# The layer's opening stage: token norm and first projections put into the kernel's own instruction order, with the gain pre_g multiplied on VectorE

## The chip, the cores and the metric

One core of a Trainium2 chip runs the whole layer. The metric is the device time of one execution in microseconds (us). Engines are named as in the profile: PE is TensorE, DVE VectorE, ACT ScalarE, POOL GpSimd, SP the engine that issues the DMAs.

## What is computed

2064 tokens (16 meta tokens and 2048 of x, 1024 wide) are normalised, projected into six streams, and run through eight heads of stick-breaking attention beside a gated linear recurrence (RG-LRU). Both groups are normalised, gated and projected back.

```
u = rmsnorm(concat(meta, x), pre_g)
q, k, v, g_att, x_lru, g_lru = split(u @ w_in)
z = q k^T / sqrt(128);  w = exp(log_sigmoid(z) + sum over later keys of log(1 - sigmoid(z)))
att = rmsnorm(w v, att_out_g) * silu(g_att)
xc = causal conv of width 4 over x_lru;  r, i = sigmoid(block gates of xc)
a = exp(8 r log_sigmoid(lambda));  h_t = a_t h_(t-1) + sqrt(1 - a_t^2) i xc
lru = rmsnorm(h, lru_out_g) * silu(g_lru)
out = x + rmsnorm(concat(att, lru) @ w_out, post_g)
```

## The kernel before

**Number format.** Every float32 operand of a matmul is split into two float16 parts, high and low, and a product is three matmuls (high by high, high by low, low by high). A projection of one 128-column block of `w_in` over n tokens is therefore 24 matmuls of n columns (8 slices of the 1024-wide sum, three products each), into one PSUM bank of the pool `psm`, which has three. `uH` and `uL` hold the normalised tokens transposed (feature on the partition), for the whole run.

**Opening stage.** The tokens come in a tile of the 16 meta tokens and 16 tiles of 128. `norm_tile` loads a tile by DMA; ACT squares it with a row sum and takes a square root (L192, L193); DVE inverts that (L194); POOL multiplies the tile by the scaled gain `pgt` (L195); ACT writes the high part, scaled by the inverse (L197), and DVE the low part (L198). The first four tiles are transposed on PE, into a PSUM tile `z` for both halves, and copied out by ACT (L205) and DVE (L206); the other 13 go through two DMA transposes each (L208, L209). `load_w` brings a weight block: DMA, a column maximum on DVE (L144, L147), a small PE matmul that spreads it over the partitions (L150), five small DVE instructions (L151 to L156), the high part on ACT (L158), the low part on DVE (L159).

Four weight blocks are needed first: k0, v0, q0 of attention head 0, and xl0, the recurrence input of channel block 0. The tokens are projected in five pieces (`KV_CH`: 144, 384, and three of 512) for k, v and q, and in six pieces of 344 for xl0. `Mix` is the recurrence of one channel block in two halves of 1032 tokens: a convolution (DVE, four instructions), six gate steps (ACT cast L485, DVE subtraction L486, two PE matmuls L496 and L497, two ACT sigmoids L498 and L499), then tanh, two exponentials, a square root, a multiply on POOL, a scan on DVE, and a square. In the opening stage the first half of block 0 is run by `lru_mix` when the last token piece is due; the second half comes later, with head 0's attention.

**What sets the order.** The opening stage is written in program order, and the framework's scheduler chooses the order of PE, ACT and DVE instructions by its own estimates. From the line `with tc.manual_schedule(...)` on, the order of these three engines is the one in which the kernel's own planner emits them: `Plan` keeps a clock per engine, `Ring` counts free buffers, `Chunk` is one projection piece, `weave` picks what PE does next (a list of urgent steps, then attention outputs, then attention scores, then the projection pieces in the list `fill`), and callbacks emit what follows on ACT and DVE. POOL's and SP's queues are set by the framework throughout. Before the planner starts, the weight blocks xl1, ga0 and gl0 are already converted (they were prefetched inside the last token piece); the planner's loader then has one raw buffer `wraw` and three converted pairs `wH`, `wL`.

Attention of a head: PE computes scores into `z` (two PSUM buffers), ACT takes the sigmoid (L305), POOL masks the diagonal (L310), DVE scans (L315), ACT and DVE split the result (L327, L333), a DMA transposes it, and PE multiplies it with v (L352).

Of the kernel before, what the change touches and what calls it, by code (L numbers as in the profile page):

```python
# [19 lines left out]
P = 128  # L20
# [50 lines left out]
def hybrid_layer(nc, tc, I, out):  # L71
# [3 lines left out]
    PE_T = 400  # L75
# [40 lines left out]
    pgt = rp.tile([P, 1036], F32, name="lrow")[:, :D]  # L116
# [13 lines left out]
    def load_w(col, home=None, raw=None):  # L130
# [11 lines left out]
        sp.dma_start(out=raw, in_=I["w_in"][col])  # L142
        m = sm.tile([P, 4], F32, name="wm", bufs=6)
# [6 lines left out]
        pe.matmul(out=ps[:, :P], lhsT=onesb, rhs=dg, start=True, stop=True)  # L150
        dve.tensor_reduce(out=m[:, 1:2], in_=ps[:, :P], axis=AX.X, op=ALU.max)  # L151
# [6 lines left out]
        act.activation(out=wH, in_=raw, func=AF.Copy, scale=m[:, 3:4])  # L158
        dve.scalar_tensor_tensor(out=wL, in0=raw, scalar=m[:, 3:4], in1=wH, op0=ALU.mult, op1=ALU.subtract)  # L159
        yield wH, wL, m[:, 2:3]  # L160

    def proj(w, c0, n):

        for ps in proj_steps(w, c0, n):
            pass
        return ps
# [18 lines left out]
    early_rows = [acc_l[:, 0:D], acc_l[:, D:2 * D]]  # L185

    def norm_tile(src, rows, t0):
        xt = early_rows.pop(0) if early_rows else frow()
        x2 = sg.tile([P, 1024], F32, name="w", bufs=N_W) if t0 // P % 2 else sg.tile([P, 1024], F32, name="wT", bufs=3)
        sp.dma_start(out=xt[:rows, :D], in_=src)  # L190
        ss = sm.tile([P, 1], F32, name="ss")
        act.activation(out=x2[:rows, :D], in_=xt[:rows, :D], func=AF.Square, accum_out=ss[:rows])  # L192
        act.activation(out=ss[:rows], in_=ss[:rows], func=AF.Sqrt, bias=eps[:rows], scale=1.0 / D)  # L193
# [6 lines left out]
        if t0 < PE_T:  # L200
            z = psz.tile([P, 2, 512], F32, name="z").bitcast(F16).rearrange("p a (k c) -> p a k c", k=KT)
            for x, t in enumerate((xh, xl)):
                for k in range(KT):
                    pe.transpose(out=z[:, x, k, :rows], in_=t[:rows, k * P:(k + 1) * P], identity=ident[:rows, :rows])
            act.copy(out=uH[:, :, t0:t0 + rows], in_=z[:, 0, :, :rows])  # L205
            dve.tensor_copy(out=uL[:, :, t0:t0 + rows], in_=z[:, 1, :, :rows])  # L206
            return
        sp.dma_start_transpose(uH[:, :, t0:t0 + rows], xh[:rows])  # L208
        sp.dma_start_transpose(uL[:, :, t0:t0 + rows], xl[:rows])  # L209


# [4 lines left out]
    def pair(ps, n, hi, lo):  # L216

        act.activation(out=hi, in_=ps[:, :n], func=AF.Copy, scale=PSC)
        dve.scalar_tensor_tensor(out=lo, in0=ps[:, :n], scalar=PSC, in1=hi, op0=ALU.mult, op1=ALU.subtract)  # L219

    def k_chunk(h, w, j, ps=None):
        if j == 0:
            kqv["kH"] = kp.tile([P, T], F16, name="kH")
            kqv["kL"] = kp.tile([P, T], F16, name="kL")
        c0, n = KV_CH[j]
        pair(ps or proj(w, c0, n), n, kqv["kH"][:, c0:c0 + n], kqv["kL"][:, c0:c0 + n])

    def q_chunk(h, w, j, ps=None):
        if j == 0:
            kqv["qH"] = kp.tile([P, S], F16, name="qH")  # L230
            kqv["qL"] = kp.tile([P, S], F16, name="qL")
        c0, n = KV_CH[j]
        if j == 0:
            c0, n = NM, n - NM
        pair(ps or proj(w, c0, n), n, kqv["qH"][:, c0 - NM:c0 - NM + n], kqv["qL"][:, c0 - NM:c0 - NM + n])

    def v_chunk(h, w, j, ps=None):


        if j == 0:  # L240
            kqv["v"] = kp.tile([P, NB, P], F16, name="v")
            kqv["vb"] = sm.tile([P, NQ], F32, name="vb", bufs=2)
            kqv["vl"] = sm.tile([P, len(KV_CH)], F32, name="vl", bufs=2)
            kqv["vu"] = unscale(w, 1.0 / VSC)
        v = kqv["v"]
        c0, n = KV_CH[j]
        a = acc_a[:, 0:1040] if h == 0 else frow()
        if j == 0:
            pool.memset(a[:, 0:1], 0.0)
        else:  # L250
            dve.tensor_copy(out=a[:, 0:1], in_=kqv["vl"][:, j - 1:j])
        act.activation(out=a[:, 1:n + 1], in_=(ps or proj(w, c0, n))[:, :n], func=AF.Copy, scale=VSC)
        dve.tensor_copy(out=kqv["vl"][:, j:j + 1], in_=a[:, n:n + 1])
        d = a[:, 520:520 + n]
        pool.tensor_tensor(out=d, in0=a[:, 0:n], in1=a[:, 1:n + 1], op=ALU.subtract)
        t = stage("sv").bitcast(F16).rearrange("p (x c) -> p x c", x=2)
        act.copy(out=t[:, 0, :n], in_=d)
        dve.tensor_tensor(out=t[:, 1, :n], in0=d, in1=t[:, 0, :n], op=ALU.subtract)
        o = 0
        if j == 0:  # L260
            tm = sm.tile([P, P], F16, name="tm", bufs=1)
            pool.memset(tm[:, 3 * NM:], 0.0)
            for x, y in enumerate((0, 0, 1)):
                dve.tensor_copy(out=tm[:, x * NM:(x + 1) * NM], in_=t[:, y, 0:NM])
            sp.dma_start_transpose(v[:, 0:1, :], tm)
            o = NM
        b0, nb = (c0 + o - NM) // P, (n - o) // P
        dve.tensor_scalar(out=kqv["vb"][:, b0:b0 + nb].unsqueeze(2),
                          in0=a[:, 1 + o:1 + n].rearrange("p (b c) -> p b c", c=P)[:, :, P - 1:P],
                          scalar1=kqv["vu"], scalar2=None, op0=ALU.mult)  # L270
        for x in range(2):
            sp.dma_start_transpose(v[:, 1 + x * NQ + b0:1 + x * NQ + b0 + nb, :], t[:, x, o:n])
# [86 lines left out]
    def attend(i, zs, o):  # L359
        pred = None  # L360
        for x in tile_segs(i):
            x.pred, pred = pred, x
            x.scores()
            x.products_1(zs)
            if x.si == 0:
                x.mask()
            x.products_2()
            x.split_1()
            x.split_2()
            x.split_3()  # L370
            x.output(o)

    def silu(ps, n, w, tag):

        g = stage(tag)
        act.activation(out=g[:, :n], in_=ps[:, :n], func=AF.Sigmoid, scale=w)
        dve.scalar_tensor_tensor(out=g[:, :n], in0=ps[:, :n], scalar=w, in1=g[:, :n], op0=ALU.mult, op1=ALU.mult)
        return g

# [14 lines left out]

    def att_gate_early(h, g, w, us):

        sp.dma_start(out=aa_d[g][h], in_=silu(proj(w, NM + 512 * g, 512), 512, us, "sa"))

    def att_gate(h, g, w, us, ot, gt=None, ps=None):
        if w is None:  # L400
            gt = gt or stage("sa")
            sp.dma_start(out=gt, in_=aa_d[g][h])
        else:
            gt = silu(ps or proj(w, NM + 512 * g, 512), 512, us, "sa")
        dve.scalar_tensor_tensor(out=gt, in0=ot, scalar=prm(ATG, h), in1=gt, op0=ALU.mult, op1=ALU.mult)
        sp.dma_start(out=aa_d[g][h], in_=gt)
# [40 lines left out]
    def lru_x(c, m, w, us, xs, ps=None):  # L447
# [9 lines left out]
        ps = ps or proj(w, half * HT + a, n)  # L457
        act.activation(out=xs[half][:, 3 + a:3 + a + n], in_=ps[:, :n], func=AF.Copy, scale=us)

    class Mix:  # L460
# [3 lines left out]
        def __init__(self, c, xs, gw, left=None):  # L464
# [81 lines left out]
    def lru_mix(c, xs, gw, left=None):  # L546
# [6 lines left out]
        for f in (mix.tanh, mix.exp_a, mix.exp_a2, mix.rest, mix.sqrt, mix.drive, mix.recur, mix.square, mix.add):  # L553
            for m in range(len(xs)):
                f(m)
# [1039 lines left out]
```

## Time and profile before

| | |
|---|---|
| median of 3 runs | 1898.63 us (1898.0 to 1902.92) |
| profiled execution | 1900.03 us, span of its instructions 1898.2 us |
| PE, DVE, ACT, POOL busy | 1796.1, 1280.7, 1043.8, 407.9 us |
| mean granted TensorE clock | 0.991 |
| longest PE line | projections, L174: three groups of about 620 us |
| last projection of k0, v0, q0, xl0 ends | 163.7 us |
| first scores of head 0, 1, 2 | 118.4, 341.1, 518.4 us |

The span is what the profile's rows cover. A granted clock of 1.0 is the full 2.4 GHz, 0.5 is 1.2 GHz. PE busy and PE idle together give the span; as PE is nearly always busy after the first 220 us, the question in a stage is what PE waits for there.

### The profile page before, as it was taken

The page shows a single profiled execution, that of the slowest core. Times are in us where ns is not written, and L with a number is a line of the kernel's source. Part 1 is how long each engine was busy: PE and PEld are TensorE (multiplying, and loading weights), DVE is VectorE, ACT ScalarE, POOL GpSimd, SP SyncE. Part 2 cuts the span into 40 slices and gives each one's busy share as a digit, 9 for nine tenths or more (in the row PEclk, how much of TensorE's full clock was granted, in tenths as well). Part 3 has the DMA queues.
Part 4 walks back from the last instruction along what each step waited for, and adds up shares of the span by engine and source line. Part 5 has one row for each costly group of instructions (what it writes and reads, how often), then busy time and mean ns, then how long its engine had stood idle before and what let it go on. Part 6 is the DMA issues. An engine that isn't in the chain of part 4 may idle for free.

```text
span 1898.2 us, 30853 instructions
## 1 busy us (share of the span) xinstructions
PE 1796.1 (95%) x12048; PEld 1151.8 (61%) x12048; DVE 1280.7 (67%) x1752; ACT 1043.8 (55%) x1775; POOL 407.9 (21%) x460
## 2 busy tenths in 40 slices
PE   2878899999999999999999999999999999999998
PEld 2434565466556655665566566556655578888776
DVE  8446886788588758866886798588757852124554
ACT  5555846756665575567456656665674743233221
POOL 4421200511140132104111411150123000002222
PEclk9989999999999999999999999999999999999999
DMA  5922561264146406631652265137404774355554
GB/s 165 199 50 58 105 130 39 62 139 92 46 96 127 95 24 130 122 73 32 131 115 62 54 136 107 54 74 140 95 30 94 197 177 138 105 163 170 177 184 138
DMA packets 435809, 205.29 MB, mean 108 GB/s; under 512 B 370368, under 2 KB 404160, under 8 KB 435664
## 3 DMA queue, kind: packets, MB, share of 16 engines
q1 hardware_dynamic: 435664, 203.33, 46.0%
q8 instruction: 94, 1.54, 0.3%
q14 instruction: 51, 0.42, 0.1%
HBM read 78.23 MB, written 34.08 MB: 59 GB/s over the span
## 4 chain that ended last, share of the span: by engine, by line
PE 73%; DVE 8%; ACT 6%; DMA 6%; issue 5%; POOL 2%; SPq 1%; DVEq 0%; POOLq 0%; ACTq 0%
PE mm L174 39%; PE y L728 18%; PE o L352 8%; PE z L301 6%; DMA wT<-w 4%; DVE row L315 2%; ACT row L305 1%; DVE lrow L531 1%; DMA wraw<-in_w_in 1%; PE mm L496 1%; DVE w L333 1%; ACT lrow L499 1%; ACT w L327 1%; ACT ot L385 1%; DMA row<-in_x 1%
## 5 line engine op out<-in xcount | busy, mean ns | idle before, releaser
L174 PE MATMUL mm<-uH,wH 128*128 128x512 f16 (+3 forms) x1808 | 620.0, 347 | 8.1 <-DVE qL L219 4.5
L174 PE MATMUL mm<-uL,wH 128*128 128x512 f16 (+3 forms) x1808 | 619.7, 346 | 2.3 <-DMA uL<-w 1.5
L174 PE MATMUL mm<-uH,wL 128*128 128x512 f16 (+3 forms) x1808 | 618.6, 346 | 2.7 <-DVE wL L159 2.7
L174 PEld LDWEIGHTS <-wH 128*128 128x128 f16 x3616 | 335.5, 99 | 287.2 <-issue 21.1
L315 DVE TENSOR_TENSOR_SCAN row<-row 128x656 f32<-128x656 f32 (+6 forms) x208 | 341.4, 1642 | 69.3 <-POOL row L310 39.8
L174 PEld LDWEIGHTS <-wL 128*128 128x128 f16 x1808 | 178.2, 99 | 164.2 <-issue 6.1
L305 ACT ACTIVATE row<-z,zs 128x656 f32<-128x656 f32 (+6 forms) x208 | 171.3, 826 | 166.7 <-PE z L301 151.6
L352 PE MATMUL o<-wT,v 128*128 128x128 f16 x3392 | 223.8, 219 | 22.0 <-DMA wT<-w 20.8
L352 PEld LDWEIGHTS <-v 128*128 128x128 f16 x3392 | 205.8, 98 | 63.0 <-issue 29.9
L333 DVE TENSOR_TENSOR w<-row,w 128x640 f16<-128x640 f32 (+5 forms) x208 | 176.2, 849 | 5.4 <-ACT w L327 5.3
L327 ACT CAST w<-row 128x640 f16<-128x640 f32 (+5 forms) x208 | 155.3, 747 | 25.9 <-DVE row L315 22.3
L310 POOL TENSOR_SCALAR_AFFINE_SELECT row<-row 128x128 f32<-128x128 f32 x128 | 88.9, 695 | 264.9 <-ACT row L305 256.7
L728 PE MATMUL y<-woH,aH 128*128 128x512 f32 x352 | 140.2, 398 | 2.0 <-DVE w L333 1.4
L728 PE MATMUL y<-woL,aH 128*128 128x512 f32 x352 | 138.0, 392 | 1.0 <-DVE woL L681 1.0
L728 PE MATMUL y<-woH,aL 128*128 128x512 f32 x352 | 138.1, 392 | 0.5 <-DVE aL L721 0.5
L301 PE MATMUL z<-kH,qH 128*128 128x328 f16 (+10 forms) x384 | 122.6, 319 | 7.6 <-ACT row L305 7.5
L301 PE MATMUL z<-kH,qL 128*128 128x328 f16 (+10 forms) x384 | 122.5, 319 | 0.0
L301 PE MATMUL z<-kL,qH 128*128 128x328 f16 (+10 forms) x384 | 122.5, 319 | 0.0
L323 POOL MEMSET w<- 128x80 f16 x128 | 21.2, 165 | 438.8 <-DMA wT<-w 331.2
L301 PEld LDWEIGHTS <-qH 128*128 128x128 f16 x768 | 72.0, 98 | 58.3 <-issue 11.2
L486 DVE TENSOR_TENSOR cs<-lrow,cs 64x344 fp32r<-64x344 f32 x96 | 49.1, 511 | 85.2 <-ACT cs L485 83.4
L1541 POOL TENSOR_TENSOR row<-row 128x512 f32<-128x512 f32 x32 | 46.5, 1454 | 261.5 <-ACT row L1540 253.6
(208 smaller groups left out, 2539.2 us busy)
## 6 DMA issues: line engine op xcount, KB each, us to landing
wraw<-in_w_in SPq DMA_DIRECT2D x46, 512.0 KB, 4.0
row<-in_x SPq DMA_DIRECT2D x31, 512.0 KB, 4.3
aa_d<-sa SPq DMA_DIRECT2D x34, 256.0 KB, 2.1
al_d<-sl SPq DMA_DIRECT2D x32, 256.0 KB, 2.7
araw<-in_w_out SPq DMA_DIRECT2D x16, 512.0 KB, 4.5
araw<-al_d SPq DMA_DIRECT2D x16, 512.0 KB, 4.3
yl_d<-ys SPq DMA_DIRECT2D x32, 256.0 KB, 2.2
row<-yl_d SPq DMA_DIRECT2D x16, 512.0 KB, 3.2
```

Of the source, the lines that this page charges most:

```text
L174: pe.matmul(out=ps[:, :n], lhsT=a[:, kt, :], rhs=b[:, kt, c0:c0 + n], start=(k == 0), stop=(k == 3 * KT - 1))
L301: pe.matmul(out=z[:, a, :n], lhsT=l[:, qs], rhs=r[:, c], start=(x == 0), stop=(x == 2))
L305: act.activation(out=self.om[:, :L].rearrange("p (a c) -> p a c", a=self.parts), in_=self.z[:, :self.parts, :self.n], func=AF.Sigmoid, sca ...
L310: pool.affine_select(out=d, in_=d, pattern=[[-1, P]], compare_op=ALU.is_gt, fill=1.0, base=0, channel_multiplier=1)
L315: dve.tensor_tensor_scan(out=om, data0=om, data1=om, initial=self.pred.om[:, 0:1] if self.si else WS, op0=ALU.mult, op1=ALU.bypass)
L323: pool.memset(w[:, 3 * NM:P], 0.0)
L327: act.copy(out=w[:, r0:r0 + nb * P], in_=om[:, self.m0:self.L])
L333: dve.tensor_tensor(out=w[:, r0 + nb * P:r0 + 2 * nb * P], in0=om[:, self.m0:self.L], in1=w[:, r0:r0 + nb * P], op=ALU.subtract)
L352: pe.matmul(out=o[:, c], lhsT=l, rhs=r, start=(self.si == 0 and x == 0), stop=(self.last and x == len(prods) - 1))
L486: dve.tensor_tensor(out=cs[oth, :n], in0=xc[own, a:a + n], in1=cs[own, :n], op=ALU.subtract)
L728: pe.matmul(out=ps, lhsT=a[:, c, :], rhs=b[:, 512 * half:512 * half + 512], start=(c == 0 and x == 0), stop=(c == KT - 1 and x == 2))
L1541: pool.tensor_tensor(out=yt[:, cs], in0=yt[:, cs], in1=pg[:, cs], op=ALU.mult)
```

## The change

The planner now starts at the first instruction. Its parts:

- **Norm on DVE.** `norm` replaces `norm_tile`. The gain is scaled once on ACT (L473, on POOL before). DVE multiplies the tile by inverse norm and gain in one instruction, in float32 and in place (L695); ACT casts the high part (L697), DVE subtracts (L700). POOL has no part in it.
- **Transposes.** The high part of 12 tiles (meta, 0 to 5, 7, 9, 11, 13, 15) and the low part of three (meta, 0, 1) go over PE, each half with a `z` tile of its own (L722, copied at L724). The other 19 go by DMA (L715). That is 120 PE transposes, 64 before.
- **Order.** ACT and DVE steps of norm and weights go through `job`, which emits, of what is ready, the tile with the lowest number first; weights v0, q0, xl0 stand among the tiles at 1.5, 2.5 and 4.5. A projection piece may start when the planner thinks that its tokens are there (`have`).
- **First LRU mix whole.** xl0 is an ordinary branch now: both halves of block 0 run their gates among the last projections, and the rest of both during head 0's attention. `lru_mix`, `prefetch` and the split into two calls are gone.
- **Decay constants.** The chain of small DVE instructions of `decay` (L418 to L434 before) is emitted when the planner's clock is at 45, and not in the first microseconds.
- **Weights.** Raw tiles of v0, q0, xl0 lie in `lrow` buffers and xl0's converted pair too (`lx`); k0, v0 and q0 hold the three converted pairs. So xl1, ga0 and gl0 are converted by the loader, one after the other, after the first of k0, v0, q0 has been used up.
- **Fill order of head 0.** All pieces of k0, v0, q0 and xl0 by token, then the four of ga0, then xl1 and gl0.

```diff
-    PE_T = 400
+    PE_HI, PE_LO = set(range(-1, 6)) | {7, 9, 11, 13, 15}, {-1, 0, 1}
-    pgt = rp.tile([P, 1036], F32, name="lrow")[:, :D]
+    pgt = acc_a[:, 0:D]
-    pool.tensor_scalar(out=pgt, in0=pgt, scalar1=gm[:, 3:4], scalar2=0.0, op0=ALU.mult, op1=ALU.add)
+    act.activation(out=pgt, in_=pgt, func=AF.Copy, scale=gm[:, 3:4])
-    def norm_tile(src, rows, t0):
...
-        dve.reciprocal(out=ss[:rows], in_=ss[:rows])
-        pool.tensor_tensor(out=xt[:rows, :D], in0=xt[:rows, :D], in1=pgt[:rows], op=ALU.mult)
-        xh, xl = x2.bitcast(F16)[:, :D], x2.bitcast(F16)[:, D:2 * D]
-        act.activation(out=xh[:rows], in_=xt[:rows, :D], func=AF.Copy, scale=ss[:rows])
-        dve.scalar_tensor_tensor(out=xl[:rows], in0=xt[:rows, :D], scalar=ss[:rows], in1=xh[:rows],
-                                 op0=ALU.mult, op1=ALU.subtract)
+            def scale():
+                dve.reciprocal(out=ss[:rows], in_=ss[:rows])
+                dve.scalar_tensor_tensor(out=x, in0=x, scalar=ss[:rows], in1=pgt[:rows], op0=ALU.mult, op1=ALU.mult)
+            J("act", t, 1.55, f, lambda t: J("dve", t, 1.4, scale, lambda t: J(
+                "act", t, 1.05, lambda: act.copy(out=d["h"], in_=x), hi)), "sqrt")
+        def hi(t):
+            J("dve", t, 1.22, lambda: dve.tensor_tensor(out=d["l"], in0=x, in1=d["h"], op=ALU.subtract), lo)
+            if i in PE_HI:
+                urgent.append((t, rz, lambda: turn(uH, "h", 0)))
+            else:
+                across(uH, "h", t)
...
+        def turn(u, a, e):
+            z = psz.tile([P, 2, 512], F32, name="z").bitcast(F16)[:, 0].rearrange("p (k c) -> p k c", k=KT)
+            for k in range(KT):
+                pe.transpose(out=z[:, k, :rows], in_=d[a][:, k * P:(k + 1) * P], identity=ident[:rows, :rows])
...
+        plan.at(45.0, lambda: (decay(), V(A(plan.free["pe"], 8, "exp"), 4500)))
...
+            if ready[self.name] > plan.free["pe"] or not have(self.c0, self.n):
...
         if h == 0:
-            return GA[:2] + XL[:3] + GL + XL[3:] + GA[2:]
+            first = branch(0) + [x for j in range(NJ) for x in (K[j], VV[j], Q[j])]
+            first.sort(key=lambda x: next(j for j, (a, n) in enumerate(KV_CH) if x.c0 + x.n <= a + n))
+            return first + GA + XL[:3] + GL + XL[3:]
...
-    for name in ("xl1", "ga0", "gl0"):
-        ready[name] = 0.0
-        rW.n -= 1
-    head[0] = {"v": [0.0] * NQ, "q": 0.0, "mix": Mix(0, xs[1:], gw, hs[0]), ...}
+    lx = row()
     with tc.manual_schedule(engines={mybir.EngineType.PE, mybir.EngineType.Activation, mybir.EngineType.DVE}):
-        loader()
-        rlrow.get(lambda: mix_start(0, 0))
+        start()
         weave()
```

How the instructions stand now is shown at three places. Names: `wm` and `dg` belong to a weight's scale, `ss` to a tile's norm, `pol` and `s` to the decay constants, `cs` to a gate step.

DVE, from the first weight's scale to the second token tile, before:

```order
L147 TENSOR_SCALAR dg<-identb,wm 128x128
L615 RECIPROCAL gm<-gm 128x1
L427 TENSOR_TENSOR pol<-pol,s_527 128x8
L194 RECIPROCAL ss<-ss 16x1
L428 TENSOR_SCALAR pol<-pol 128x8
L151 TENSOR_REDUCE wm<-mm 128x1
...
L144 TENSOR_REDUCE wm<-lrow 128x1
...
L159 SCALAR_TENSOR_TENSOR wL<-wraw,wm,wH 128x1024
L147 TENSOR_SCALAR dg<-identb,wm 128x128
L428 TENSOR_SCALAR pol<-pol 128x8
...
L144 TENSOR_REDUCE wm<-lrow 128x1
...
L198 SCALAR_TENSOR_TENSOR wT<-acc_l,ss,wT 16x1024
```

and in the change:

```order
L149 TENSOR_SCALAR dg<-identb,wm 128x128
L472 RECIPROCAL gm<-gm 128x1
...
L694 RECIPROCAL ss<-ss 16x1
L695 SCALAR_TENSOR_TENSOR acc_l<-acc_l,ss,acc_a 16x1024
L163 SCALAR_TENSOR_TENSOR wL<-wraw,wm,wH 128x1024
...
L695 SCALAR_TENSOR_TENSOR acc_l<-acc_l,ss,acc_a 128x1024
L700 TENSOR_TENSOR w<-acc_l,w 16x1024
...
L695 SCALAR_TENSOR_TENSOR acc_a<-acc_a,ss 128x1024
...
L700 TENSOR_TENSOR wT<-acc_l,wT 128x1024
L700 TENSOR_TENSOR w<-acc_a,w 128x1024
L146 TENSOR_REDUCE wm<-lrow 128x1
L149 TENSOR_SCALAR dg<-identb,wm 128x128
```

The decay chain (L427, L428) and the second and third weight's maximum (L144) stood between the first tiles; now the first three tiles' multiply and subtraction follow each other, with the second weight's maximum behind them.

PE, from the last token piece to the scores of head 0, before:

```order
L174 MATMUL mm<-uH,lrow 128x344
L496 MATMUL mm<-cs_1003,gH 128x344
L497 MATMUL mm<-cs_1003,gL 128x344
L301 MATMUL z<-kH,qH 128x144
...
L496 MATMUL mm<-cs_1012,gH 128x344
L497 MATMUL mm<-cs_1012,gL 128x344
L496 MATMUL mm<-cs_1020,gH 128x344
L497 MATMUL mm<-cs_1020,gL 128x344
L496 MATMUL mm<-cs_1028,gH 128x344
L497 MATMUL mm<-cs_1028,gL 128x344
...
L174 MATMUL mm<-uH,wH 128x512
```

and in the change (the last rows of a projection, then a gate step, a further piece of it, and the end of all projections):

```order
L174 MATMUL mm<-uH,wL 128x512
L379 MATMUL mm<-cs_1220,gH 128x344
L380 MATMUL mm<-cs_1220,gL 128x344
L174 MATMUL mm<-uH,wH 128x512
...
L379 MATMUL mm<-cs_1223,gH 128x344
L380 MATMUL mm<-cs_1223,gL 128x344
...
L174 MATMUL mm<-uH,wL 128x512
L152 MATMUL mm<-dg,onesb 128x128
L379 MATMUL mm<-cs_1256,gH 128x344
L380 MATMUL mm<-cs_1256,gL 128x344
L219 MATMUL z<-kH,qH 128x144
```

Before, the gate steps of the first half stand in one row, one behind the other, ahead of the last token piece of k, v and q. Now each stands alone among the projection matmuls, eight ahead of the first scores' place and four around them.

ACT, from the first scores of head 0 to the high part of ga0's weight, in the change:

```order
L223 ACTIVATE row<-z,zs 128x144
L161 ACTIVATE wH<-wraw,wm 128x1024
L381 ACTIVATE row<-mm,pp 64x344
...
L223 ACTIVATE row<-z,zs 128x400
...
L390 ACTIVATE row<-row,nsp 128x1032 x2
...
L393 ACT_TABLE_LOAD
L393 ACTIVATE lrow<-row,nsp_m 128x1032
L223 ACT_TABLE_LOAD
L223 ACTIVATE row<-z,zs 128x528
L397 ACT_TABLE_LOAD
L397 ACTIVATE row<-row,nsp_m_76 128x1032
L161 ACTIVATE wH<-wraw,wm 128x1024
```

The high part of ga0 (the last row) comes behind the tanh of both halves and two exponentials of the first, with table loads between them. Before, ga0 had been converted ahead of the first of these sigmoids but one.

## Rows read from the trace of the kernel before

**Rows 1.** The page: busy time of each engine, and PE's busy tenths in 40 slices.

```profile
PE 1796.1 (95%) x12048; PEld 1151.8 (61%) x12048; DVE 1280.7 (67%) x1752; ACT 1043.8 (55%) x1775; POOL 407.9 (21%) x460
...
PE   2878899999999999999999999999999999999998
```

**Rows 2.** Busy time by stretch; the columns stand in the first line.

```profile
core 0: us, PE busy (x) PEld busy (x) DVE busy (x) ACT busy (x) POOL busy (x), PEclk, DMA share, GB/s
0.00:35.49 35.49, 5.06 (x51) 3.99 (x52) 29.85 (x62) 19.13 (x31) 17.39 (x19) 1.00 0.46 169
35.49:97.40 61.91, 48.55 (x308) 29.58 (x307) 37.84 (x71) 35.53 (x63) 31.27 (x16) 0.94 0.90 188
...
118.40:164.00 45.60, 31.51 (x139) 15.43 (x139) 18.82 (x33) 24.88 (x35) 7.67 (x6) 0.81 0.14 41
164.00:220.00 56.00, 48.98 (x374) 31.42 (x372) 41.99 (x53) 49.60 (x84) 16.70 (x22) 1.00 0.33 58
...
341.11:518.38 177.27, 168.56 (x1250) 102.52 (x1249) 138.86 (x181) 110.74 (x187) 44.10 (x48) 1.00 0.42 90
```

**Rows 3.** What PE waited for until 164 us: us in total, times, longest.

```profile
PE mm L150 <- DVE dg L147: 28.6, 4, 11.4
PE mm L496 <- DVE cs L486: 5.2, 4, 3.2
...
PE mm L174 <- DVE qL L219: 4.5, 1, 4.5
```

**Rows 4.** Timeline of POOL: start us, us, instruction, idle time before it and its releaser.

```profile
9.62 4.64 POOL L195 TENSOR_TENSOR acc_l<-acc_l,lrow 16x1024 f32<-16x1024 f32 x2
17.35 4.88 POOL L195 TENSOR_TENSOR row<-row,lrow 128x1024 f32<-128x1024 f32 x2 [3.10 <-ACT w L192]
```

**Rows 5.** Timeline of DVE, 0 to 40 us.

```profile
3.66 0.17 DVE L423 TENSOR_TENSOR s<-y 128x8 f32<-128x8 f32 x1
...
9.91 4.38 DVE L428 TENSOR_SCALAR pol<-pol 128x8 f32<-128x8 f32 x1
...
16.42 1.28 DVE L159 SCALAR_TENSOR_TENSOR wL<-wraw,wm,wH 128x1024 f16<-128x1024 f32 x1
17.61 2.34 DVE L147 TENSOR_SCALAR dg<-identb,wm 128x128 bf16<-128x128 bf16 x1
...
23.57 1.27 DVE L198 SCALAR_TENSOR_TENSOR wT<-acc_l,ss,wT 16x1024 f16<-16x1024 f32 x1
```

**Rows 6.** Timeline of ACT, 0 to 40 us.

```profile
6.98 1.05 ACT L192 ACTIVATE wT<-acc_l 16x1024 f32<-16x1024 f32 x1 [4.00 <-DMA acc_l<-in_meta]
...
8.21 1.28 ACT L193 ACT_TABLE_LOAD   x1
9.51 0.29 ACT L193 ACTIVATE ss<-ss,eps 16x1 f32<-16x1 f32 x1
...
17.18 1.13 ACT L197 ACTIVATE wT<-acc_l,ss 16x1024 f16<-16x1024 f32 x1
```

**Rows 7.** Timeline of PE: the first projection matmul.

```profile
35.49 0.33 PE L174 MATMUL mm<-uH,wH 128*128 128x144 f16 x1
```

**Rows 8.** Chain that ended last, 130 to 170 us: start us, us, what.

```profile
141.65 3.73 DMA wraw<-in_w_in
...
150.04 1.30 DVE wL L159
151.35 3.64 DMA wraw<-in_w_in
...
166.10 1.94 PE mm L174 x9
```

**Rows 9.** Timeline of ACT: the two sigmoids of a gate step.

```profile
120.11 0.54 ACT L498 ACTIVATE row<-mm,pp 64x344 f32<-64x344 f32 x1
120.67 0.54 ACT L499 ACTIVATE lrow<-mm,pp 64x344 f32<-64x344 f32 x1
```

**Rows 10.** Timeline of PE: a wait among head 0's scores.

```profile
205.03 0.30 PE L301 MATMUL z<-kH,qH 128*128 128x320 f16 x1 [2.86 <-ACT row L305]
```

More of the change, by code (lines that the diff above doesn't have):

```diff
@@ L214, in hybrid_layer @@
     kqv = {}
[L216 to L272, printed above, removed]
@@ L357, in tile_segs @@
         return [Seg(i, si, *t, len(segs)) for si, t in enumerate(segs)]
[L359 to L378, printed above, removed]
     def att_out(h, g, o, vsc):
@@ L393, in att_out @@
         return ot
[L395 to L406, printed above, removed]
     HT = T // 2
@@ L779, in due, with job, end, ready @@
             while self.todo and self.todo[0][0] <= self.free["pe"]:
-                heapq.heappop(self.todo)[2]()
-        def flush(self):
-            while self.todo:
-                t, _, f = heapq.heappop(self.todo)
-                self.free["pe"] = max(self.free["pe"], t)
-                f()
+                self.t, _, f = heapq.heappop(self.todo)
+                f()
+        def job(self, e, prio, t, us, f, then, table=None):
+            def end(t):
+                t = self.run(e, t, us, table)
+                self.at(t, lambda: then(t))
+            if prio is None:
+                f()
+                end(t)
+                return
+            def ready():
+                heapq.heappush(self.jobs[e], (prio, self.n, f, end))
+                self.n += 1
+                self.at(max(self.free[e], self.t), lambda: self.pick(e))
+            self.at(t, ready)
+        def pick(self, e):
+            if not self.jobs[e]:
+                return
+            if self.free[e] <= self.t + 0.01:
+                _, _, f, end = heapq.heappop(self.jobs[e])
+                f()
+                end(self.t)
+            self.at(self.free[e], lambda: self.pick(e))
     plan = Plan()
@@ L830, in loader, with mm @@
-        rW.get(lambda: rraw.get(raw_free))
+        parts = load_w(ctile[name[:-1]] + int(name[-1]), home, raw)
+        next(parts)
+        J = lambda e, t, us, then: plan.job(e, prio, t, us, lambda: next(parts), then)
+        t = (LD if prio is None else LDX)(plan.free["pe"])
+        plan.at(t, lambda: J("dve", t, 1.45, lambda t: urgent.append((t + (3.0 if prio is None else 0.0), rmm, mm))))
+        def mm():
+            next(parts)
+            J("dve", PE(0, 128), 1.2, lambda t: (rmm.put(t), J("act", t, 1.1, lambda t: J("dve", t, 1.25, end))))
@@ new lines, in have, with start @@
+    def have(c0, n):
+        return all(ut.get(i, 1e9) <= plan.free["pe"] for i in range((c0 - NM) // P, (c0 + n - NM - 1) // P + 1))
+    def start():
+        rrow.n -= 2
+        homes.extend(frow() for _ in range(2))
+        rW.n -= 3
+        rraw.n -= 1
+        weight(None, None, rraw.put, -2)
+        norm(-1)
+        rlrow.n -= 4
+        for i in range(3):
+            weight(lx if i == 2 else None, row(), rlrow.put, (1.5, 2.5, 4.5)[i])
+        plan.at(45.0, lambda: (decay(), V(A(plan.free["pe"], 8, "exp"), 4500)))
+        loader()
@@ L833, in hybrid_layer, with __init__ @@
     class Chunk:
-        def __init__(self, name, c0, n, then, gate=None, first=None, last=False):
+        def __init__(self, name, c0, n, then, gate=None, first=None, last=False, home=None):
             self.name, self.c0, self.n, self.then, self.gate, self.first, self.last = name, c0, n, then, gate, first, last
+            self.home = home or rW
             self.steps = None
@@ L1158, in recur @@
             if m + 1 == n:
-                head[c]["hs"] = ([mix.left] if n == 1 else []) + mix.xcs
+                head[c]["hs"] = mix.xcs
             plan.at(t, lambda: square(m))
```

218 lines of the change are left out of this document (87 added, 131 removed).

## The prediction, made before the changed kernel was run

> **What bounds the kernel now.** I read the page first [rows 1]: PE is busy 95% of the span, and of its 40 slices of 47 us only the first four stand clearly below nine tenths. The end is set by PE's work and by what PE loses in the first 220 us. The table by stretch [rows 2] says where: 5.06 us busy of the first 35.49, then 48.55 of 61.91, 31.51 of the 45.60 up to the last projection of k0, v0, q0 and xl0, and 48.98 of the next 56.00. The idle times add up to 30.4 + 13.4 + 14.1 + 7.0 = 65 us, and the granted clock is 0.94 and 0.81 in the second and third, so that part of the busy time there is at 1.2 GHz. In the steady stretch of head 1 PE misses only 8.7 of 177.
>
> PE's waits [rows 3] name VectorE: 28.6 us in four waits for `dg`, the step that spreads a weight's maximum, 5.2 us for the gate steps' `cs`, 4.5 us for one `qL`. The timelines of POOL and DVE, side by side [rows 4, 5], tell why `dg` is late. POOL's gain multiply takes 4.64 us for two tiles. An eight-element DVE instruction that starts 0.3 us after them takes 4.38 us and ends with them, where the same kind takes 0.17 alone, and `dg` takes 2.34 us beside the next two. So DVE is busy 29.85 us of the first 35.49 without having 29.85 us of work.
>
> **The change part by part.** All sums are made against the profiled execution, 1900.0 us, which is 1.4 us above the median of the runs.
>
> *Start.* The first projection matmul stands at 35.5 us [rows 7]. In the change, ACT ends the meta tile's root at 9.8 and scales the gain, 1.1 us like its other 1024-element instructions [rows 6]: 10.9. Up to k0's first piece, DVE then has eight instructions of 1024 elements (three multiplies, three subtractions, k0's low part, v0's maximum). Such an instruction keeps DVE for 1.2 us, from L159's start to the next one's [rows 5]: 9.6 us, and with `dg` and the copies of three low transposes some 11. ACT has eight of 1.1 us beside it. First projection at about 22: 13 us earlier.
>
> The new multiply itself (float32 out, two tensors and a scalar in) has no row. The nearest is L198, with the same operands and 1.27 us [rows 5]; the far end is POOL's rate, 2.32 us [rows 4]. I take 1.2 from start to start. At the far end 17 tiles cost another 19 us of DVE. Multiply and subtraction at 1.2 each are 41 us for 17 tiles; the four weights need 13, convolution, gate splits, evictions and copies 28, the decay chain of 31 small instructions 6 (0.17 each plus a gap): 88 us of DVE until the projections end. They end after 130 us by the sum below, so DVE has room as a whole, though not at the start.
>
> *Up to xl0.* From 22 us DVE has 14 long instructions (three more maxima and low parts among norm steps of tiles 2 to 6) before xl0's low part is there: 17 us, with three groups of small scale instructions 3, evictions 1.5, and some 4 us of waits for ACT and PE in queue order. xl0's first piece starts at about 47. PE does only the 144-token pieces and transposes until then.
>
> *The projections.* From there PE is the bound. Left are 1920 columns of each of k0, v0, q0 and 2064 of xl0, 24 matmuls per column; nine matmuls of 512 take 1.94 us [rows 8], 0.42 ns a column: 79.2 us. Five blocks of eight transposes are 2.2 and eight gate steps 2.3. (All 56 added transposes are 3.0 us of PE.) For a low clock at first and for waits in queue order I add 5. The last projection ends at 47 + 89 = 136, not 163.7: 28 us earlier. Tokens are not late: the last tile's subtraction is due near 87 by DVE's queue without waits, with some 4 us for its DMA transpose behind it, and PE wants it at about 115. SP's loads of tiles 7 on stand behind these transposes, which this slack covers. The decay chain now falls at about 50, beside k0's and v0's 384-token pieces; without that cover it would cost its 6 us.
>
> *A wait comes new.* The pieces of ga0 follow, and ga0 is not converted yet. xl1's small PE matmul stands behind the last projection (the order shows it), so its low part ends near 139 and only then is the raw buffer free. ga0's load takes 3.7 us [rows 8], maximum and scale 2.5: 145.5. Its high part stands on ACT behind the rest of the gate steps (two sigmoids of 0.54 each [rows 9]), head 0's first sigmoids and splits, two tanh and two exponentials of 1.1, and three table loads of 1.28 [rows 6]: 15 us from 138, so 153, and with high and low part 155.5. PE has 5 us of attention and gates in these 19. Without ACT's share it would be 149: two conversions follow each other at about ten us in the rows [rows 8]. Before, ga0's first matmul stood at 163.7, so 8 us are left; and by then PE has done the second half's six gate steps (1.7 us) and 3.4 us more of attention. That makes 13 us ahead.
>
> *Behind it.* The 7.0 us idle of 164 to 220 [rows 2] come from ACT's table loads for the second half, one wait of 2.86 us for a sigmoid among them [rows 10]. In the change more of these loads fall into the wait for ga0, and four ga0 pieces of 5.2 us are there to run. I leave 2 us: 5 saved. From head 1's end on the order of PE has as many instructions per head as before; nothing changes.
>
> Sum: 13 + 5 = 18 us. 1900.0 - 18 is 1882 for a profiled execution, **1880 us** for the median.
>
> **A rule against it.** Rows first: in the opening stage DVE is the helper with most to do [rows 2], and this change puts 17 multiplies of 1.2 us on it. The Trainium skill, Perfetto Trace Analysis, section Optimizing Scalar/DVE Operations, says that a saturated DVE may be relieved by giving work to ScalarE or even GpSimd, though it warns that those two share a port. By the first half of that rule the change goes the wrong way: it is rival 1. By the second half the move out of GpSimd costs DVE less than it looks. The trace agrees with the second half in the two stretched instructions above; no run yet shows the first.
>
> **The rivals.**
> 1. *VectorE sets the pace.* If DVE's queue rather than PE is the limit throughout, the 17 x 1.2 = 20 us lie on the path and eat the gain: 1880 + 20 = 1900, no change. For it: PE already waits for DVE in all of [rows 3], and up to xl0 DVE is the limit. Against it: 88 us of work in 130.
> 2. *Slower: the gate steps hold PE.* PE's queue now has 12 gate steps singly among projections and first scores, each behind an ACT cast and a DVE subtraction that stand in line with the norm of the last tiles. A late `cs` stops the projections behind it. The longest such wait was 3.2 us [rows 3]; 12 of them are 38 us, 35 beyond what the sum holds: 1915. At 2.3 us per step the result would be slower by over 0.3%. Against it: four of them cost 5.2 in all, and projection matmuls stand between as cover.
> 3. *ga0 is in time.* If ACT takes ga0's high part without that delay, at 149, the sum gains 6.5: 1873.5; with no waits in queue order among the projections either, 1868.5; and with nothing lost behind it, 1866. Against it: the order on ACT is fixed.
> 4. *Half of it.* The start's alternation of ACT and DVE costs more than the few us that I gave it, xl0 comes at 56 and not 47: 1889. The change doing less than it says is excluded by the order.
>
> **How the numbers follow.** Forecast 0.52, rival 1 0.12, rival 2 0.09, rival 3 0.18, rival 4 0.09. A measurement of this kernel can tell about 0.3% (5.7 us) from no change. Faster by more: the forecast and rivals 3 and 4, 0.79; same: rival 1, 0.12; slower: rival 2, 0.09. The range runs from rival 3's far end, with 3 us for the start, to rival 1: 1863 to 1900; it leaves out rival 2 and less than that below.
>
> **What would show it.** First projection matmul near 22 us, xl0's first piece near 47, last projection near 136, ga0's first matmul near 155 with a gap of over ten us before it, no DVE instruction of eight elements beyond half a us in the first 40 us, and the scores of head 2 some 18 us before 518.4. Wrong would be: PE waits for `cs` beyond 20 us in sum, DVE without idle time up to the last projection, or a head later than the second that takes longer than before.

## The result, and the profile after

| | before | after |
|---|---|---|
| median | 1899.24 us (1898.0 to 1902.92, 4 runs) | 1883.22 us (1882.76 to 1883.62, 4 runs) |
| profiled execution | 1900.03 us | 1882.98 us |
| span of its instructions | 1898.2 us | 1881.1 us |
| first scores of head 0, 1, 2 | 118.4, 341.1, 518.4 us | 134.7, 316.1, 495.9 us |

The ratio is 0.9912, with a 95% interval of 0.9895 to 0.993. The page of the changed kernel, busy time of each engine and PE's busy tenths:

```profile
PE 1795.0 (95%) x12104; PEld 1155.2 (61%) x12104; DVE 1282.7 (68%) x1759; ACT 1047.9 (56%) x1789; POOL 343.3 (18%) x442
...
PE   3987999999999999998999899999999999999998
```

Against [rows 1] POOL lost 64.6 us of busy time, DVE gained 2.0, and PE is busy 1.1 us less, with 56 more transposes. So 16.0 of the 17.1 us by which the span got shorter are time in which PE stood idle before. The table by stretch shows where it still does, the columns as in [rows 2]:

```profile
0.00:20.00 20.00, 3.56 (x40) 2.92 (x40) 12.97 (x23) 13.18 (x19) 1.41 (x12) 1.00 0.84 303
20.00:40.00 20.00, 10.39 (x111) 8.92 (x109) 18.26 (x41) 17.43 (x32) 0.62 (x3) 0.80 0.50 126
40.00:60.00 20.00, 15.79 (x95) 9.39 (x96) 17.96 (x53) 15.61 (x25) 0.29 (x1) 0.77 0.57 143
60.00:80.00 20.00, 20.00 (x126) 11.48 (x125) 17.29 (x21) 12.31 (x21) 1.41 (x1) 1.00 1.23 231
80.00:100.00 20.00, 17.93 (x98) 9.82 (x97) 8.41 (x15) 17.55 (x30) 1.30 (x3) 1.00 0.16 34
100.00:120.00 20.00, 19.69 (x113) 10.72 (x113) 8.66 (x10) 10.50 (x18) 4.12 (x3) 1.00 0.28 54
120.00:140.00 20.00, 17.02 (x85) 8.27 (x82) 11.07 (x20) 12.65 (x24) 1.33 (x2) 1.00 0.07 14
140.00:160.00 20.00, 9.78 (x53) 5.84 (x54) 13.54 (x25) 18.52 (x27) 4.68 (x8) 0.66 0.29 78
```

There are two holes. One is the first 60 us, where DVE is busy 18 of 20 from 20 us on. The other is 140 to 160, where PE misses 10.2 us, ACT is busy 18.5 of 20, and the granted clock is 0.66. The longest of PE's waits from 0 to 220 us name the same things (us in total, times, longest):

```profile
PE mm L152 <- DVE dg L149: 13.1, 3, 8.3
PE z L722 <- ACT w L697: 12.6, 4, 5.8
PE o L270 <- DMA wT<-w: 8.1, 3, 5.1
PE mm L379 <- DVE cs L369: 3.2, 2, 2.0
```

The 28.6 us for `dg` of [rows 3] are 13.1, and the gate steps' 5.2 are 3.2, although all twelve now run before 141 us and only six did before 164. The steps that the prediction named, on PE's timeline of the changed kernel: the first projection, xl0's first piece (its first two matmuls need only the high part and stand at 43.20; it goes on at 46.00, when the low part is there), head 0's first scores (right after the last projection), two attention outputs, and ga0's first matmul:

```profile
21.55 0.32 PE L174 MATMUL mm<-uH,wH 128*128 128x144 f16 x1
...
46.00 0.75 PE L174 MATMUL mm<-uH,lrow 128*128 128x344 f16 x2 [2.05 <-DVE lrow L163]
...
134.73 0.24 PE L219 MATMUL z<-kH,qH 128*128 128x144 f16 x1
...
145.88 0.58 PE L270 MATMUL o<-wT,v 128*128 128x128 f16 x4 [5.06 <-DMA wT<-w]
...
151.82 1.22 PE L270 MATMUL o<-wT,v 128*128 128x128 f16 x10 [2.17 <-DMA wT<-w]
...
155.75 0.39 PE L174 MATMUL mm<-uH,wH 128*128 128x512 f16 x1 [1.07 <-ACT wH L161]
```

So the front came as the working had it. What the working did not have lies behind head 2. Here are the stretches from one head's first scores to the next, heads 2 to 4 of the kernel before and then of the changed one (columns as above):

```profile
518.38:696.75 178.37, 176.62 (x1296) 106.51 (x1294) 137.17 (x189) 109.78 (x191) 39.35 (x51) 1.00 0.44 90
696.75:875.41 178.66, 176.63 (x1296) 106.45 (x1294) 136.28 (x189) 109.42 (x191) 39.34 (x51) 1.00 0.44 90
875.41:1056.47 181.06, 178.15 (x1297) 107.26 (x1295) 136.21 (x189) 109.67 (x191) 39.07 (x51) 0.99 0.43 89
```

```profile
495.91:674.96 179.05, 176.23 (x1296) 106.74 (x1295) 136.82 (x189) 107.77 (x188) 36.74 (x51) 1.00 0.43 90
674.96:857.77 182.81, 178.64 (x1296) 107.07 (x1295) 138.84 (x188) 106.97 (x188) 37.45 (x51) 0.99 0.43 88
857.77:1039.72 181.95, 176.40 (x1295) 106.63 (x1294) 136.97 (x190) 107.76 (x188) 35.70 (x50) 1.00 0.45 89
```

The number of PE instructions in a head is the same but for one or two, the time is not. At head 2 the changed kernel leads by 518.38 - 495.91 = 22.5 us. At head 7 it leads by 1414.10 - 1400.18 = 13.9, so 8.6 are gone, and the tail (484.1 before, 480.9 after) gives 3.2 back: 17.1 in the span. PE idles 20.0 us in heads 2 to 6 of the changed kernel and 11.1 in those of the kernel before, so the loss is idle time. It can be seen on PE's timeline of the changed kernel, in heads 3 and 4, all the idle times over 1.2 us:

```profile
703.45 0.72 PE L270 MATMUL o<-wT,v 128*128 128x128 f16 x10 [1.97 <-DMA wT<-w]
710.36 1.07 PE L270 MATMUL o<-wT,v 128*128 128x128 f16 x16 [1.75 <-DMA wT<-w]
...
886.01 0.89 PE L270 MATMUL o<-wT,v 128*128 128x128 f16 x13 [2.08 <-DMA wT<-w]
892.93 1.07 PE L270 MATMUL o<-wT,v 128*128 128x128 f16 x16 [2.79 <-DMA wT<-w]
```

An attention output reads `wT`, the weights that a DMA has transposed. Before, there is one such wait per head (at 726.96 in head 3, 1.45 us), now there are two. Half of what head 3 alone loses is something else: PE is busy 2.0 us longer in it, at a granted clock of 0.99. From 704.4 us, behind the wait of 1.97, the clock stands at 0.5 for 3.4 us. The kernel before has the same dip in head 4 (178.15 busy).

### The profile page after: what moved, and what is told of

Its sections match the earlier page's. It is cut to its first block, busy times and chain, and to the rows that moved or that the text cites. A ratio compares the mean times of both kernels' runs of the same rounds, so it can differ in the third digit from the quotient of the medians.

```text
span 1881.1 us, 30861 instructions
## 1 busy us (share of the span) xinstructions
PE 1795.0 (95%) x12104; PEld 1155.2 (61%) x12104; DVE 1282.7 (68%) x1759; ACT 1047.9 (56%) x1789; POOL 343.3 (18%) x442
## 5 line engine op out<-in xcount | busy, mean ns | idle before, releaser
L174 PEld LDWEIGHTS <-wH 128*128 128x128 f16 x3616 | 333.9, 98 | 273.1 <-issue 10.4
L233 DVE TENSOR_TENSOR_SCAN row<-row 128x656 f32<-128x656 f32 (+6 forms) x208 | 352.4, 1695 | 131.9 <-POOL row L228 101.5
L228 POOL TENSOR_SCALAR_AFFINE_SELECT row<-row 128x128 f32<-128x128 f32 x128 | 59.9, 469 | 406.4 <-ACT row L223 374.7
L530 DVE TENSOR_TENSOR aL<-araw,aH 128x1024 fp32r<-128x1024 f32 x32 | 39.4, 1231 | 93.2 <-ACT aH L527 92.1
```

Source lines behind the costliest of these rows:

```text
L228: pool.affine_select(out=d, in_=d, pattern=[[-1, P]], compare_op=ALU.is_gt, fill=1.0, base=0, channel_multiplier=1)
L233: dve.tensor_tensor_scan(out=om, data0=om, data1=om, initial=self.pred.om[:, 0:1] if self.si else WS, op0=ALU.mult, op1=ALU.bypass)
L530: dve.tensor_tensor(out=aL, in0=raw, in1=aH, op=ALU.subtract)
```

## The experiments

Medians are of three or more runs; a ratio is to the kernel before on the same chip. Diffs are against the changed kernel unless they say otherwise.

**Which half of the change pays.** The multiply back on POOL, in the changed kernel's order:

```diff
-                dve.scalar_tensor_tensor(out=x, in0=x, scalar=ss[:rows], in1=pgt[:rows], ...)
+                pool.tensor_tensor(out=x, in0=x, in1=pgt[:rows], op=ALU.mult)
...
+                t = plan.run("pool", t, 2.35)
```

> The changed kernel with one part undone: POOL multiplies the tile by the gain again, ACT scales the high part, DVE the low one; the planner is told of POOL's 2.35 us, and all else stays. My theory, that POOL's multiply costs by its own length and by holding up DVE: the first projection comes at 26 to 30 us and not near 22, eight-element or 128-column DVE instructions of over 2 us are back, and the time is 1889 to 1895. Rival, that the order alone makes the gain and the engine of the multiply is a swap: within 2 us of 1883.

Measured: 1893.66 us, ratio 0.9963 (0.9949 to 0.9976). Its first projection is at 28.69, not 21.55. DVE's timeline there, one instruction:

```profile
12.35 9.33 DVE L163 SCALAR_TENSOR_TENSOR wL<-wraw,wm,wH 128x1024 f16<-128x1024 f32 x1 [1.93 <-ACT wH L161]
```

and POOL's timeline beside it:

```profile
11.36 4.64 POOL L695 TENSOR_TENSOR acc_l<-acc_l,acc_a 16x1024 f32<-16x1024 f32 x2 [9.39 <-ACT acc_a L473]
15.97 2.33 POOL L695 TENSOR_TENSOR acc_a<-acc_a 128x1024 f32<-128x1024 f32 x1
18.27 2.33 POOL L695 TENSOR_TENSOR row<-row,acc_a 128x1024 f32<-128x1024 f32 x1
```

A subtraction that takes 1.28 us by itself [rows 5] takes 9.33 here: it ends 1.1 us after the last of four POOL multiplies that follow each other without a gap (the first row holds two).

The other half alone, the kernel before with only the multiply moved (diff against that):

```diff
-        pool.tensor_tensor(out=xt[:rows, :D], in0=xt[:rows, :D], in1=pgt[:rows], op=ALU.mult)
+        dve.scalar_tensor_tensor(out=xt[:rows, :D], in0=xt[:rows, :D], scalar=ss[:rows], in1=pgt[:rows],
+                                 op0=ALU.mult, op1=ALU.mult)
```

> The kernel before with that one part alone: the multiply by inverse norm and gain on DVE in one instruction, ACT casts, DVE subtracts; the framework still sets the order. My theory: DVE's stretched instructions go, the first projection comes at 24 to 28 us and not 35.5, but the stretch from 118 to 160 us (gate steps in a row, weights one by one) stays as it is, so 4 to 10 us are gained: 1889 to 1895. Rival, that DVE sets the pace of the opening: 1899 or more.

> The kernel before with the gain on DVE once more, with more rounds, since its first runs lay 12 us apart. If it really has most of the change's gain without the new order: 1883 to 1888. If the first median was luck: above 1890.

Measured: 1886.44 us (1879.87 to 1892.16), ratio 0.9927 (0.99 to 0.9955), and once more 1887.65 (1884.02 to 1889.08), 0.9931 (0.9917 to 0.9944). The first projection stands at 21.88, as early as in the changed kernel, and heads 1 and 2 come 15.5 and 15.7 us sooner than before. DVE's timeline of the kernel before shows where the start's 13.6 us lay, with three more instructions like those of [rows 5]:

```profile
20.06 2.19 DVE L427 TENSOR_TENSOR pol<-pol,s 128x8 f32<-128x8 f32 x1
...
26.80 2.32 DVE L428 TENSOR_SCALAR pol<-pol 128x8 f32<-128x8 f32 x1
...
29.63 2.30 DVE L429 TENSOR_TENSOR pol<-pol,y 128x8 f32<-128x8 f32 x1
```

With the 4.38 and 2.34 of [rows 5] these five took 13.5 us, 12.6 more than their kind takes alone (0.15 to 0.26 each), and DVE stood idle for 0.14 us in all from 9.83 us to the first projection at 35.49. In the run with the multiply on DVE none of its instructions takes over 1.3 us up to 100 us. So the hold-up by itself accounts for nearly all that the start won; no run parts it from the multiply's own length on POOL (2.33 us against 1.28).

So of the 16 us the multiply gives 12 to 14 by itself and the order 6 to 7 by itself; on top of the multiply, the order adds 3 to 4, which is little more than these runs' scatter can tell. In the profiles this small sum hides larger parts: against the multiply alone, the changed kernel leads by 6.7 us at head 2, by nothing at head 7 (1400.18 against 1399.90), and its tail gives 3.4. The working never parted the two, and by its terms one would have given the order, which moves xl0's first matmul from 57.95 in this run to 43.20, a larger share.

**The wait for ga0.** Loader order ga0, xl1, gl0:

```diff
-    order[4:7] = ["xl1", "ga0", "gl0"]
+    order[4:7] = ["ga0", "xl1", "gl0"]
```

> The changed kernel with ga0 ahead of xl1 in the list of weights, so that ga0 is the first block converted after the opening. My theory, that PE stands still between the last projection (135 us) and ga0's first matmul (156 us) because ga0 waits for xl1's conversion: ga0's first matmul comes at about 141, and 8 to 11 us are gained: 1872 to 1875. Rival, that ACT's queue behind head 0's first sigmoids and table loads is what PE really waits for there: the gap shrinks but the time comes back later, 1880 to 1884.

Measured: 1897.25 us, ratio 0.9987 (0.9977 to 0.9997), 14 us slower than the change; neither expectation had it. ga0 is in time (142.38), and PE's timeline shows two other waits in its place, with idle times and releasers:

```profile
179.93 1.89 PE L270 MATMUL o<-wT,v 128*128 128x128 f16 x16 [7.34 <-DMA wT<-w]
193.00 0.45 PE L174 MATMUL mm<-uH,wH 128*128 128x344 f16 x1 [6.62 <-ACT lrow L341]
```

Head 2 starts at 501.69, 5.8 us later than in the changed kernel, and the five heads from there to head 7 take 8.6 us more in sum. My reading is that ga0's pieces were the cover for those outputs and, run earlier, no longer stand there; no run shows that by itself.

**Transposes and decay chain.** The transposes as before, high and low parts of the meta tile and tiles 0 to 2 over PE:

```diff
-    PE_HI, PE_LO = set(range(-1, 6)) | {7, 9, 11, 13, 15}, {-1, 0, 1}
+    PE_HI, PE_LO = set(range(-1, 3)), set(range(-1, 3))
```

> The changed kernel with the transposes of before: both halves of meta and tiles 0 to 2 on PE, all others by DMA. My theory, that the added PE transposes are worth little: 2.4 us less of PE work and seven ACT copies of 1 us fewer, against high halves that come some 3 us later where PE is the bound anyway: 1880 to 1886. Rival, that the high half over PE is what makes the tokens come in time: 1888 to 1893, with PE waiting for uH.

Measured: 1884.70 us, ratio 0.9918 (0.9903 to 0.9933), as expected. The 56 added transposes change nothing that can be told.

The decay chain at the start again:

```diff
-        plan.at(45.0, lambda: (decay(), V(A(plan.free["pe"], 8, "exp"), 4500)))
+        decay()
+        V(A(2.5, 8, "exp"), 4500)
```

> The changed kernel with the chain of small DVE instructions for the decay constants emitted ahead of everything, not at 45 us of the planner's clock. My theory, that the opening is one chain through DVE up to xl0's weight and that the decay chain costs its 6 us there but nothing beside the projections: first projection and xl0's first piece 3 to 6 us later, time 1886 to 1889. Rival, that these 31 instructions fill DVE's waits for the first loads: within 2 us of 1883.

Measured: 1885.16 us, ratio 0.992 (0.9905 to 0.9935), 2 us more than the change, between the two expectations and hardly clear of noise. The chain then lies at 2.6 to 11.4 us, in part where DVE waits for loads anyway, and the first projection does not come later for it (20.97 us). xl0's first matmul comes 3.2 us later (46.35), its low part 1.9 (47.87), and the first scores 1.0.

**What is lost behind head 2.** The runs above tell which half of the change it belongs to. Here are heads 3 and 4 with the planner's order and the multiply on POOL, then with the order of before and the multiply on DVE:

```profile
685.37:868.49 183.12, 178.09 (x1296) 107.52 (x1295) 138.59 (x188) 106.89 (x188) 37.24 (x51) 0.99 0.41 88
868.49:1051.36 182.87, 178.08 (x1295) 107.16 (x1294) 137.12 (x190) 107.64 (x188) 35.93 (x50) 0.99 0.44 88
```

```profile
680.78:859.21 178.43, 176.62 (x1297) 106.45 (x1295) 137.42 (x189) 109.67 (x191) 39.39 (x51) 1.00 0.43 90
859.21:1040.08 180.87, 178.28 (x1295) 107.20 (x1294) 136.35 (x189) 109.54 (x191) 38.99 (x51) 0.99 0.42 89
```

The longer heads go with the planner's order and not with the multiply. PE's timelines agree: with the multiply alone, heads 2 to 6 keep the order of PE's steps that they had in the kernel before, one and the same in every head; with the multiply back on POOL they have that of the changed kernel, in which two orders alternate from head 3 on. Which part of the new opening does this, no run shows.

The planner takes an output's weights as there some time after the DMA transpose was planned. The constant was 1.0 us:

```diff
-            x.ready += 1.0
+            x.ready += 2.5
```

> The changed kernel with one number of the planner changed: it takes the transposed products of attention as ready 2.5 us after its own estimate of their DMA, not 1.0. In the change, PE waits 3 to 6 us per head in heads 3 to 6 for these transposes (1.7 in the kernel before). My theory, that the new order of the later heads puts the outputs too close behind their DMA: these waits fall below 2 us per head and 5 to 8 us are gained: 1875 to 1878. Rival, that the waits belong to the DMA or to buffers and only move: 1881 to 1885.

Measured: 1877.89 us, ratio 0.9883 (0.987 to 0.9897), as the theory had it. From 500 to 1400 us PE waits for transposed weights 2.0 us, against 14.6 in the changed kernel. With 2.0:

> The changed kernel with the outputs' delay at 2.0 us, between 1.0 (1883.2) and 2.5 (1877.9); 4.0 gave 1903.6. Theory (the delay is a real one, and the heads get better the nearer it is to what the transposed weights take): 1877 to 1881. Rival (each value only drops the planner into another order of the heads, which may be a good or a bad one, as 2.5 did in the kernel before): the time is not between the two, below 1875 or above 1886, and the head lengths behind head 2 are not near 179 to 180 each.

Measured: 1866.39 us (1864.55 to 1868.04), ratio 0.9816 (0.9803 to 0.983): the fastest kernel of this study, 17 us below the change. It lies below what the theory named, where the rival had it. Its heads 3 and 4:

```profile
672.06:850.43 178.37, 176.49 (x1297) 106.81 (x1295) 137.60 (x189) 106.84 (x190) 37.78 (x51) 1.00 0.44 90
850.43:1027.31 176.88, 176.51 (x1296) 106.76 (x1295) 137.58 (x189) 107.03 (x190) 37.62 (x51) 1.00 0.45 91
```

PE is busy for 176.5 of 177 to 178. With 4.0:

> The changed kernel with the outputs' delay at 4.0 us in place of 2.5. Theory: at 2.5 only 2.0 us of waits for the transposed weights were left from 300 to 1400, so nothing is left to win: 1876 to 1880. Rival (the later outputs push the end of each head back): 1881 to 1886.

Measured: 1903.56 us, ratio 1.0007 (0.9998 to 1.0015); both theories missed. What PE waits for from 500 to 1400 us, first with 1.0, then with 2.0, then with 4.0 (us in total, times, longest):

```profile
PE o L270 <- DMA wT<-w: 14.6, 10, 2.8
PE o L270 <- ACT sq L285: 3.4, 1, 3.4
PE mm L379 <- DVE kL L796: 1.4, 5, 0.3
```

```profile
PE o L270 <- DMA wT<-w: 4.7, 6, 1.4
PE o L270 <- ACT ot L282: 0.5, 3, 0.2
```

```profile
PE o L270 <- ACT ot L282: 14.4, 5, 3.3
PE mm L174 <- ACT lrow L382: 7.7, 10, 0.9
PE mm L379 <- DVE sa L892: 6.0, 5, 1.2
PE mm L152 <- DVE dg L149: 4.1, 5, 0.8
PE o L270 <- DMA wT<-w: 0.6, 1, 0.6
```

Too early, and an output waits for its weights; too late, and it waits for ACT to take the previous output out of its bank (`ot`), and PE waits too for ACT's gate sigmoids (`lrow`), for DVE's evictions (`sa`) and for a weight's scale. Is 2.5 simply the better value? The kernel before with it (the same line, diff against that):

> The kernel before with the outputs' assumed delay at 2.5 us in place of 1.0, nothing else. Theory (what the changed kernel lost behind head 2 is a wait for the transposed weights that this delay sets, and the kernel before pays less of it: 12.3 us from 300 to 1400 against 18.2 us): a gain of 3 to 6 us, 1893 to 1896. Rival (the delay of 2.5 is simply the better one for every order, and worth as much here as in the changed kernel): 5 to 8 us or more, 1891 to 1894, with waits for the transposed weights under 3 us from 300 to 1400 either way.

Measured: 1908.28 us, ratio 1.0037 (1.0023 to 1.005): slower, which neither theory had. Nor did the wait go: from 300 to 1400 us PE waits 10.4 us for transposed weights, where both had under 3 (12.3 with 1.0). And the kernel before with the multiply on DVE and 2.5:

> The kernel before with the multiply on VectorE and the outputs' delay at 2.5 us: own order of the opening not in it. Theory (the opening in the planner's order still is worth its 3 to 4 us once the waits behind head 2 are gone from both): 1881 to 1884, against 1878 with the whole change. Rival (order is worth more, since the changed kernel was the one that lost behind head 2): 1885 to 1889. Second rival (it is worth nothing): 1876 to 1880.

Measured: 1894.45 us, ratio 0.9962 (0.995 to 0.9974), 7 to 8 us slower than with 1.0; none of the three had it. In both, the heads fall into pairs. Heads 3 and 4 of the kernel before with 2.5:

```profile
693.48:880.62 187.14, 178.33 (x1296) 108.16 (x1294) 145.09 (x193) 115.66 (x197) 48.04 (x55) 0.99 0.40 86
880.62:1057.93 177.31, 175.90 (x1297) 107.06 (x1294) 126.85 (x186) 101.81 (x184) 26.39 (x46) 1.00 0.42 91
```

DVE and ACT work of one head now falls into its neighbour (145 and 127 us of DVE, 136 and 136 before), and the head with more of it is 8.5 us longer than it was. So the constant does two things: in the changed kernel it sets a real wait (14.6, 4.7, 2.0 and 0.6 us for transposed weights at 1.0, 2.0, 2.5 and 4.0), and in both it drops the planner into one repeating order of the heads or another. The second is my reading of why the same value wins 5 us in one kernel and costs 6 in the other; no run holds the order and moves the wait alone. Which value suits the kernel before was not tried beyond these two.

**The loader.** Weights converted in whole stages (three pieces with DVE, ACT, DVE in one go, as before) and not by single steps in the job queue:

```diff
-            rW.get(lambda: rraw.get(lambda: weight(None, None, done)))
+            rW.get(lambda: rraw.get(lambda: weight_whole(done)))
```

> The changed kernel with the loader's weight blocks (xl1, ga0 and all later ones) emitted in three pieces, as before, and not in six with a turn for each. My theory, that the finer steps changed the order of the later heads and with it the 3 to 4 us that heads 3 to 6 lose each: these heads come back to 178.5 us and the time is 1872 to 1878. Rival, that the order of the later heads follows from where the planner's clock stands when they begin, however weights are emitted: heads of 180 us and more, 1881 to 1890.

Measured: 1923.97 us, ratio 1.0127 (1.0113 to 1.0141), far outside what was expected. Head 1 starts 8.7 us later than in the changed kernel and head 2 34.2 later; from 130 to 530 us PE waits:

```profile
PE z L219 <- ACT row L223: 18.0, 6, 4.7
PE o L270 <- DMA wT<-w: 13.0, 8, 5.1
```

Attention scores wait for ACT's sigmoids, 18.0 us in all; in the changed kernel that wait is 0.6 us there. Its later heads run in pairs as well. Why the sigmoids are late there was not followed up.

## Why the prediction was right, and where not

The forecast was 1880 us, 1863 to 1900; it came to 1883.2. The opening went by the mechanism that the working gave; that the total came so near was luck in part. Step by step:

- *Start*: 22 us for the first projection, 21.55 measured. The multiply has its row now, 1.28 us and 1.2 from start to start, as taken. The eight-element instructions of the decay chain (48 to 53 us now) take 0.17 to 0.20 each, none is stretched.
- *Up to xl0*: 47, by the low part, measured 46.00; the first matmuls, with the high part alone, stand at 43.20.
- *The projections*: last one at 136, measured 134.3. The DMA transposes are not late: PE has no wait for them up to there. The slack was smaller than in the working, though: the last tile's subtraction, due near 87 by DVE's queue, ends at 109.4, since its steps on ACT stand behind gate steps.
- *A wait comes new*: ga0 at 155.5, measured 155.75, by the path described (high part on ACT at 154.56, behind table loads). The gap before it is not one of over ten us, though. In 140 to 160 us PE's 10.2 idle us are divided among outputs that wait for their transposed weights (5.06 and 2.17 of them) and ga0. The working had no wait for these outputs there.
- *Decay chain*: "without that cover it would cost its 6 us". The run gives about 2, since the first microseconds have cover of their own. That term was too large; it stood in no sum.
- *Behind it*: from ga0's start to 220 us PE idles 3.4 us, where the working left 2 of the 7.0. The step that failed is "From head 1's end on the order of PE has as many instructions per head as before; nothing changes." The count is the same, the order is not, and with the order the outputs' waits differ. Heads 2 to 6 lost 8.6 us, all behind the line that I had drawn. The sign that I gave for wrong, "a head later than the second that takes longer than before", is there: 182.81 us against 178.66. What hid this in the total is that the lead at head 2 is more than the 18: 22.5 us. Of these, 17.0 come from the front and 5.5 are head 1's own, which idled 8.7 us before [rows 2] and idles 179.79 - 176.54 = 3.3 now: its outputs and scores waited 4.1 and 3.1 us and wait 0.2 and 0.6. (Head 1 is no shorter for it, 179.79 against 177.27, since 8.0 us of PE work that stood ahead of it before stand in it now.) The working took head 1's loss as steady and had no term for it. So the time is near the forecast because two errors cancel, +4.5 and -5.4 (8.6 less the 3.2 that the tail gave).

The rivals. *VectorE sets the pace* is excluded: DVE is busy 8.4 and 8.7 of 20 us between 80 and 120. Here the Trainium skill's page Perfetto Trace Analysis, section Optimizing Scalar/DVE Operations, by which a saturated DVE may be relieved by giving work to GpSimd, with a warning that the two share a port, was weighed before; the run with the multiply given back to GpSimd is 10.4 us slower (1893.66 against 1883.22), although DVE is the busiest helper in the first 60 us of the changed kernel, so here the warning counts. *The gate steps hold PE* is excluded by 3.2 us in all for `cs`. *ga0 in time* was priced at 1866 to 1873.5 by its place on PE alone; the run that brings it in time, by putting xl1 behind it, is at 1897. By my reading the price left out what ga0's pieces cover when they come later; no run brings ga0 forward with xl1 left in its place. *Half of it*, with xl0 at 56, is excluded by xl0's 43.20 and 46.00.

## What to carry to other kernels

Where POOL and DVE work on the same stage, look at DVE's shortest instructions: one that takes far longer than its size beside a POOL instruction shows that the two engines are not parallel there, and a POOL step moved to DVE can cost less than it frees. Where a planner with estimates sets the order, no stage is finished with its own end: another plan for the front can give every later stage another order (the 15.7 us that the multiply alone won at the front, outside the plan, left the later order as it was), so a forecast has to compare the order itself and not the number of instructions. And a planner's constant for a transfer is worth a scan of some values after each larger change, since a value that helps in one order can hurt in another (in the changed kernel 17 us lie between 1.0 and 2.0, and 37 between 2.0 and 4.0).

## What the runs showed of the hardware

A DVE instruction held up by POOL can wait for more than one POOL instruction. In the run with the multiply on POOL, one DVE subtraction of 1024 elements took 9.33 us and ended only after four POOL multiplies, 9.24 us from the first one's start to the last one's end. It need not wait so long: in the kernel before, `dg` at 17.61 us [rows 5] ended at 19.95, 2.3 us before the second of the two multiplies beside it did [rows 4]. The Trainium skill, SBUF — State Buffer, section SBUF: two separate sides, says that the two engines' shared port pair is held for a whole instruction and that the other engine blocks. The trace agrees that DVE stands still, and shows it for a run of POOL instructions without a gap as well as for a single one. When DVE gets in between two of them, these runs leave open.
